# Row maxima and reciprocal sums of an attention kernel sent through DRAM instead of through TensorE transposes

## The chip, the cores and the metric

One core of a Trainium2 chip runs the whole program. The metric is the device time of one execution in microseconds. The engines named below are TensorE (PE; PEld is its weight load), VectorE (DVE), ScalarE (ACT), GpSimd (POOL) and SyncE (SP), whose queue only issues DMAs here. SBUF and PSUM tiles have 128 partitions.

## The reference

The program is a two-layer diffusion backbone over 2048 latent and 256 context tokens. Each layer normalizes, projects to three groups of heads, runs attention, a short convolution and a conformer module, and projects back. The part that matters here is the attention and the gate that follows:

```python
def one_block(qi):
    s = jnp.einsum('bqhd,bkhd->bhqk', qi, k).astype(jnp.float32) * sm_scale
    p = jax.nn.softmax(s, axis=-1).astype(v.dtype)
    return jnp.einsum('bhqk,bkhd->bqhd', p, v)
...
y_a = attn * jax.nn.silu(g_a)
...
return jnp.concatenate([y_a, y_b, y_c], axis=-1)
```

There are 8 heads of 96 numbers for a query or key (64 plus 32 rotary) and 64 for a value. Latent queries attend to all 2304 tokens, context queries to the 256 context tokens only. In the last layer only latent queries are needed.

## The kernel before

Products that need full precision are made of two halves of each operand (a rounded high part and the rest), three matmuls for one product. A layer runs in stages: tokens, features, `attention`, `project`. The order of instructions on every engine is set ahead of time by a scheduler that works on priorities and on its own estimates; a block written inside `tc.high_priority` comes earlier than the code around it.

**Attention.** The work is cut into blocks of one head and 512 queries: 32 per layer, and in layer 0 one more of 256 context queries per head. For each block the key tiles come in pairs. The scores stand with keys on partitions and queries along the row (`sc`, three matmuls, L1073 to L1075), ScalarE makes the exponentials twice (L1076, L1077), GpSimd makes the low half (L1078), and TensorE multiplies with the values (`po`, L1100, L1101). VectorE adds the exponentials up (`acc`, L1085).

The exponent needs the maximum of each query's scores. `prepare` finds it: for each of a block's four tiles of 128 queries, and each of five stretches of keys (four of 512, one of 256), a matmul `pmax` puts queries on partitions (L985) and VectorE reduces along the row (L986); `finish` takes the negated maximum of the five (L989). The result stands as one number per partition. The score matmul wants it as a row, since row 96 of `Q` is multiplied by a row of ones in `K`. So `turn` multiplies the tile `mx`, whose column 96 holds the maxima and whose other columns are zero, by the identity (L994, four matmuls `pmt`) and ScalarE copies partition 96 of the result into row 96 of `Q` (L995). `pmax` has two PSUM buffers, and `pmt` shares one with the transposes below.

`ahead` deals these steps out over the pairs of the block before: LEAD says how many pairs early. They have a higher priority than the pairs. `load` brings `K`, `Q` and the values of the next head on POOL's queue.

When a block is finished, `close` (L1103 on) copies `acc` and `po` out of PSUM, stores `po` to `o_d` on SP's queue (L1108), turns `acc` by four transposes (`psum_t`, L1113), reduces (L1115) and writes the reciprocal of each query's sum into the tile `rinv` (L1116), again one number per partition.

**Projection.** `prepare_y` makes the operand of the output projection for a block of 512 tokens. For each pair of heads it loads `yr`, `ylo` and `yg` on SP's queue (the two halves of the attention's output and the gate), spreads the reciprocals of two heads over 64 columns each (`rr`, ScalarE, L1174), transposes them (`prr`, TensorE, L1175), and VectorE adds the halves (L1176), multiplies by the reciprocals (L1177) and by the gate (L1178). The first block of `prepare_y` is written at a high priority and runs into the end of the attention. In layer 0, SP's queue also issues the 512 KB loads of modulation weights (`wm`) during attention.

## Time and profile before

| | us |
|---|---|
| median of 3 runs | 3695.93 |
| lowest and highest | 3688.89, 3696.3 |
| the profiled execution, time | 3695.0 |
| the profiled execution, span | 3693.2 |
| TensorE busy | 3529.8 (96%) |
| VectorE busy | 2888.8 (78%) |
| POOL busy | 2341.6 (63%) |
| ScalarE busy | 2166.7 (59%) |
| mean granted clock of TensorE | 0.978 of full |

All rows below come from the profiled execution. Its span runs from the first to the last instruction; its time has 1.8 us more around that. Layer 0's attention lies at about 740 to 1600 us, layer 1's at about 2640 to 3400. A busy time of TensorE is made from modelled ends of pipelined matmuls; the cost of a matmul is read from the distance between starts.

### The profile page before, as it was taken

The numbers are of one execution on the slowest core, as the hardware profiler recorded it, in microseconds if no ns is written. First come the engines' busy times: TensorE is split into PE (matmuls) and PEld (weight loads), VectorE is DVE, ScalarE is ACT, GpSimd is POOL, SyncE is SP. The second block draws the span as 40 slices with busy tenths as digits, with TensorE's granted clock in tenths as the row PEclk, the third lists the DMA queues.
The fourth block names the chain that finished last, engine by engine and source line by source line (L and its number), as shares of the span: only waits on it lengthen the run. The fifth ranks groups of instructions, "written<-read, shape, count | busy, mean of one in ns | idle before, by whom it ended". The sixth has DMA issues, their size and how long they took to land. (4 is left out here: it accounts for less than half of the span.)

```text
span 3693.2 us, 52810 instructions
## 1 busy us (share of the span) xinstructions
PE 3529.8 (96%) x17532; PEld 2916.9 (79%) x17532; DVE 2888.8 (78%) x5472; ACT 2166.7 (59%) x4328; POOL 2341.6 (63%) x1497
## 2 busy tenths in 40 slices
PE   7899999999999999999999989999999999998999
PEld 5787888887888787877788878887777777776777
DVE  5986977877888888888437878769988888888832
ACT  4665343247778777877445663433677777776720
POOL 4664344348888888877435654444687887877721
PEclk8999999999999999999999999999999999999999
DMA  7567333433333213312776773435232202222163
GB/s 219 171 186 205 82 107 110 113 112 78 79 79 88 61 45 82 85 58 64 232 231 207 215 213 100 114 99 125 80 76 61 41 27 61 59 61 75 43 197 114
DMA packets 394386, 411.47 MB, mean 111 GB/s; under 512 B 19168, under 2 KB 332128, under 8 KB 388960
## 3 DMA queue, kind: packets, MB, share of 16 engines
q1 hardware_dynamic: 387712, 333.87, 31.2%
q0 software_dynamic: 6400, 74.22, 8.9%
q8 instruction: 138, 2.26, 0.3%
q14 instruction: 136, 1.11, 0.1%
HBM read 266.72 MB, written 141.59 MB: 111 GB/s over the span
## 5 line engine op out<-in xcount | busy, mean ns | idle before, releaser
L1078 POOL TENSOR_TENSOR pl<-p,ph 128x1024 fp32r<-128x1024 f32 (+1 forms) x584 | 1387.2, 2397 | 276.2 <-ACT ph L1077 110.4
L986 DVE TENSOR_REDUCE mx<-pmax 128x1 fp32r<-128x512 f32 (+1 forms) x1296 | 795.1, 628 | 122.0 <-PE pmax L985 113.6
L1076 ACT ACTIVATE p<-sc 128x512 f32<-128x512 f32 x1168 | 713.4, 612 | 240.5 <-PE sc L1075 232.7
L1085 DVE TENSOR_TENSOR acc<-acc,p 128x512 f32<-128x512 f32 x1096 | 756.7, 690 | 55.9 <-ACT p L1076 29.5
L1077 ACT ACTIVATE ph<-sc 128x512 fp32r<-128x512 f32 x1168 | 703.8, 612 | 20.1 <-PE po L1100 16.2
L194 PE MATMUL pf<-hhf,wh 128*128 128x256 f32 (+1 forms) x1584 | 549.3, 348 | 18.2 <-ACT tg L867 8.4
L196 PE MATMUL pf<-hhf,wl 128*128 128x512 f32 (+1 forms) x1584 | 546.4, 347 | 4.5 <-POOL wl L191 3.7
L195 PE MATMUL pf<-hlf,wh 128*128 128x256 f32 (+1 forms) x1584 | 547.2, 346 | 0.0
L985 PE MATMUL pmax<-K,Q 96*128 96x512 f32 (+1 forms) x1296 | 465.0, 386 | 34.8 <-DVE mx L986 26.8
L1073 PE MATMUL sc<-Q,K 97*128 97x512 f32 x1168 | 476.5, 408 | 11.7 <-ACT ph L1077 9.3
L1101 PE MATMUL po<-pl,Vt 128*128 128x512 f32 x1168 | 467.9, 401 | 2.1 <-POOL pl L1078 1.8
L1074 PE MATMUL sc<-Q,K 96*128 96x512 f32 x1168 | 465.2, 398 | 0.0
L1100 PE MATMUL po<-ph,Vt 128*128 128x512 f32 x1168 | 461.9, 396 | 1.1 <-DMA Vt<-v_d 0.8
L1075 PE MATMUL sc<-Q,K 96*128 96x512 f32 x1168 | 462.4, 396 | 0.0
L191 POOL TENSOR_TENSOR wl<-wraw,wh 128x1024 fp32r<-128x1024 f32 x104 | 253.8, 2441 | 292.8 <-ACT wh L190 279.4
L747 DVE SCALAR_TENSOR_TENSOR cacc<-z,hv,cacc 128x384 f32<-128x384 f32 (+5 forms) x780 | 403.0, 561 | 14.3 <-ACT cacc L742 11.2
L194 PEld LDWEIGHTS pf<-hhf,wh 128*128 128x128 f32 x1584 | 303.7, 192 | 57.2 <-ACT wh L190 9.1
L196 PEld LDWEIGHTS pf<-hhf,wl 128*128 128x128 f32 x1584 | 303.0, 192 | 44.3 <-POOL wl L191 7.2
L985 PEld LDWEIGHTS pmax<-K,Q 96*128 96x128 f32 x1296 | 245.3, 190 | 116.9 <-DVE mx L986 58.6
L195 PEld LDWEIGHTS pf<-hlf,wh 128*128 128x128 f32 x1584 | 303.8, 192 | 36.1
L1073 PEld LDWEIGHTS sc<-Q,K 97*128 97x128 f32 x1168 | 222.2, 190 | 71.3 <-ACT ph L1077 20.0
L1075 PEld LDWEIGHTS sc<-Q,K 96*128 96x128 f32 x1168 | 224.5, 192 | 51.5
(257 smaller groups left out, 6189.0 us busy)
## 6 DMA issues: line engine op xcount, KB each, us to landing
wraw<-in_w_in SPq DMA_DIRECT2D x108, 512.0 KB
q_d<-sg SPq DMA_DIRECT2D x68, 384.0 KB
wm<-in_w_mod SPq DMA_DIRECT2D x46, 512.0 KB
v_d<-vs SPq DMA_DIRECT2D x36, 512.0 KB
kn_d<-sg SPq DMA_DIRECT2D x72, 256.0 KB
K<-kn_d POOLq DMA_DIRECT2D x16, 1152.0 KB, 8.5
Vt<-v_d POOLq DMA_DIRECT2D x16, 1152.0 KB, 14.8
o_d<-o SPq DMA_DIRECT2D x64, 256.0 KB
```

What stands on the lines that cost most here:

```text
L194: PE.matmul(out_, lhsT=ahi, rhs=bhi, start=first, stop=False)
L195: PE.matmul(out_, lhsT=ahi, rhs=blo, start=False, stop=False)
L196: PE.matmul(out_, lhsT=alo, rhs=bhi, start=False, stop=last)
L985: PE.matmul(pm[:, :w], lhsT=Q[0:QK, s // P + t, 0], rhs=K[0:QK, a // P : (a + w) // P, 0], start=True, stop=True)
L986: V.tensor_reduce(part[:, t, c : c + 1], pm[:, :w], axis=AX.X, op=ALU.max)
L1073: PE.matmul(sc[:, :n], lhsT=K[0:97, kt, 0], rhs=Q[0:97, qt, 0], start=True, stop=False)
L1075: PE.matmul(sc[:, :n], lhsT=K[0:QK, kt, 1], rhs=Q[0:QK, qt, 0], start=False, stop=True)
L1076: S.activation(p[:, z, :n], sc[:, :n], AF.Exp, scale=scale)
L1077: S.activation(ph[:, z, :n], sc[:, :n], AF.Exp, scale=scale)
L1078: G.tensor_tensor(pl[:, :, :n], p[:, :, :n], ph[:, :, :n].bitcast(F32), op=ALU.subtract)
L1085: V.tensor_tensor(acc[:, :n], acc[:, :n], p[:, z, :n], op=ALU.add)
L1101: PE.matmul(po[:, :n], lhsT=Vt[:, kt0 + z, :], rhs=pl[:, z, :n], start=False, stop=final and z == 1)
```

## The change

The maxima no longer pass through TensorE. `finish` writes them to a tile `mn` of 128 partitions x 4, SP's queue writes these 512 numbers to a row of a DRAM tensor `m_d`, one number of 4 bytes at a time, and then reads the row into `Q`. LEAD goes from 3 to 4. The reciprocals go to a small tile `ri` and by SP's queue into `r_d` in DRAM; `prepare_y` reads a row of it into 64 partitions, twice, as `rb`. The sum of the halves and its product with `rb` now stand in PSUM (`py`). The zeroed columns of `mx` are not needed any more.

```diff
-    mx = [cst.tile([P, 4, 97], F32R, name=f"mx{i}") for i in range(2)]
...
+    mx = [(cst.tile([P, 4, 5], F32, name=f"mx{i}"), cst.tile([P, 4], F32R, name=f"mn{i}")) for i in range(2)]
...
+    m_d = [dr.tile([H, NT], F32, name=f"m_d{l}") for l in range(DEPTH)]
+    r_d = [dr.tile([H, NT], F32, name=f"r_d{l}") for l in range(DEPTH)]
...
             def finish():
-                V.tensor_reduce(m[:, 0:nq, 96:97], part[:, 0:nq, 0 : len(keys)], axis=AX.X, op=ALU.max, negate=True)
+                V.tensor_reduce(m[:, 0:nq], part[:, 0:nq, 0 : len(keys)], axis=AX.X, op=ALU.max, negate=True)
 
             def turn():
-                px = psum("b" if early else "e", "pmt")
-                for t in range(nq):
-                    PE.matmul(px[0:97, t * P : (t + 1) * P], lhsT=m[:, t, :], rhs=idr, start=True, stop=True)
-                S.copy(Q[96:97, s // P : (s + n) // P, 0], px[96:97, :n].rearrange("p (a t) -> p a t", t=P))
+
+                row = m_d[l][h, s : s + n]
+                nc.sync.dma_start(row.rearrange("(t p) -> p t", p=P), m[:, 0:nq].bitcast(F32))
+                nc.sync.dma_start(Q[96:97, s // P : (s + n) // P, 0].bitcast(F32), row.rearrange("(o t p) -> o t p", o=1, p=P))
...
-        LEAD = 3
+        LEAD = 4
...
-                    V.reciprocal(rinv[l][:, s // P : s // P + nq, h], sm[:, :nq])
+                    ri = tp.tile([P, 4], F32, tag="ri", name="ri", bufs=2)
+                    V.reciprocal(ri[:, :nq], sm[:, :nq])
+                    nc.sync.dma_start(r_d[l][h, s : s + n].rearrange("(t p) -> p t", p=P), ri[:, :nq])
...
-                    px = psum("b" if bi == 0 else "cde"[k % 3], "prr")
-                    for t in range(n // P):
-                        rr = rp.tile([P, 2, 64], F32, tag="rr", name="rr", bufs=RR)
-                        S.copy(rr, rinv[l][:, s // P + t, 2 * k : 2 * k + 2].unsqueeze(2).to_broadcast([P, 2, 64]))
-                        PE.transpose(out=px[:, t * P : (t + 1) * P], in_=rr.rearrange("p a b -> p (a b)"), identity=idn)
-                    V.tensor_tensor(r[:, :n], r[:, :n], lo[:, :n], op=ALU.add)
-                    V.tensor_tensor(r[:, :n], px[:, :n], r[:, :n], op=ALU.mult)
-                    V.tensor_tensor(r[:, :n], r[:, :n], g[:, :n], op=ALU.mult)
+                    rb = rp.tile([P, 512], F32, tag="rb", name="rb", bufs=2)
+                    for z in range(2):
+                        nc.sync.dma_start(rb[64 * z : 64 * z + 64, :n], r_d[l][2 * k + z : 2 * k + z + 1, s : s + n].to_broadcast([64, n]))
+                    px = psum("b" if bi == 0 else "cde"[k % 3], "py")
+                    V.tensor_tensor(px[:, :n], r[:, :n], lo[:, :n], op=ALU.add)
+                    V.tensor_tensor(px[:, :n], px[:, :n], rb[:, :n], op=ALU.mult)
+                    V.tensor_tensor(r[:, :n], px[:, :n], g[:, :n], op=ALU.mult)
```

The order on the engines moves with it. In the new code the maxima matmul is L980, the score matmul L1068, the value matmuls L1095 and L1096, the transposes of the sums L1108; a count at a row's end (x4) stands for equal rows in sequence.

On TensorE, before, at a boundary of blocks in layer 1: the narrow `pmax` is the last of its block, and the first `sc` of that block stands at the end.

```order
L985 MATMUL pmax<-K,Q 128x256
L985 MATMUL pmax<-K,Q 128x512 x2
L994 MATMUL pmt<-idr,mx_89 97x128 x4
L985 MATMUL pmax<-K,Q 128x512
L1073 MATMUL sc<-Q,K 128x512
```

The same kind of place in the changed kernel, also layer 1.

```order
L980 MATMUL pmax<-K,Q 128x256
L1108 MATMUL psum_t<-idr,accs 128x128 x4
L980 MATMUL pmax<-K,Q 128x512 x2
L1096 MATMUL po<-pl,Vt 128x512
L1095 MATMUL po<-ph,Vt 128x512
L1096 MATMUL po<-pl,Vt 128x512
L980 MATMUL pmax<-K,Q 128x512 x2
L980 MATMUL pmax<-K,Q 128x256
L980 MATMUL pmax<-K,Q 128x512 x2
L1068 MATMUL sc<-Q,K 128x512
```

The turns are gone, and with the larger LEAD more of the next block's `pmax` and three value matmuls stand between a block's last `pmax` and its first `sc`.

On TensorE of the changed kernel there is a longer run of `pmax` in layer 1, ahead of the second block of every second head; this is its end.

```order
L980 MATMUL pmax<-K,Q 128x512 x2
L1096 MATMUL po<-pl,Vt 128x512
L1095 MATMUL po<-ph,Vt 128x512
L1096 MATMUL po<-pl,Vt 128x512
L980 MATMUL pmax<-K,Q 128x512 x2
L980 MATMUL pmax<-K,Q 128x256
L980 MATMUL pmax<-K,Q 128x512 x4
L980 MATMUL pmax<-K,Q 128x256
L980 MATMUL pmax<-K,Q 128x512
L1068 MATMUL sc<-Q,K 128x512
```

With the rows ahead of these, sixteen `pmax` of the block after stand between a block's last `pmax` and its first `sc`.

On SP's queue of the changed kernel, in layer 1's attention: `m_d<-mn` is the write of the maxima, `Q<-m_d` the read of the row, `r_d<-ri` the store of the reciprocals.

```order
L1113 DMA r_d_114<-ri 128x4x1
L989 DMA m_d_112<-mn_92 128x4x1
L1103 DMA o_d_106<-o 128x512
L990 DMA Q<-m_d_112 1x4x128
L1113 DMA r_d_114<-ri 128x4x1
L989 DMA m_d_112<-mn_90 128x4x1
L990 DMA Q<-m_d_112 1x4x128
L1113 DMA r_d_114<-ri 128x4x1
L1103 DMA o_d_106<-o 128x512
```

Before, SP's queue held only the stores of `o_d` there; now the write and the read stand in it, with a store between them at some blocks.

## Rows read from the trace of the kernel before

**Rows 1.** The page's part 1: busy us (share) and instructions by engine.

```profile
PE 3529.8 (96%) x17532; PEld 2916.9 (79%) x17532; DVE 2888.8 (78%) x5472; ACT 2166.7 (59%) x4328; POOL 2341.6 (63%) x1497
```

**Rows 2.** Windows: length, busy PE, PEld, DVE, ACT, POOL, clock, DMA.

```profile
740.00:1600.00 860.00, 854.76 (x4272) 693.94 (x4271) 738.15 (x1364) 637.18 (x1186) 708.78 (x329) 1.00 0.31 76
2640.00:3500.00 860.00, 835.70 (x3638) 660.64 (x3638) 757.06 (x1272) 643.78 (x1238) 683.16 (x311) 0.98 0.24 57
3390.00:3400.00 10.00, 7.79 (x22) 6.17 (x23) 8.01 (x11) 3.53 (x7) 3.67 (x2) 0.66 0.42 120
```

**Rows 3.** Waits in 2749 to 3373: us in total, times, longest.

```profile
PEld pmax L985 <- DVE mx L986: 21.9, 61, 0.6
PEld sc L1073 <- ACT Q L995: 2.0, 5, 0.4
```

**Rows 4.** Timeline of PE, layer 1: start us, us, instruction.

```profile
3020.69 0.28 PE L985 MATMUL pmax<-K,Q 96*128 96x256 f32 x1
...
3021.83 0.49 PE L994 MATMUL pmt<-idr,mx 128*97 128x128 f32 x4
3022.20 0.50 PE L1101 MATMUL po<-pl,Vt 128*128 128x512 f32 x1
...
3022.99 0.40 PE L985 MATMUL pmax<-K,Q 96*128 96x512 f32 x1
3023.23 0.40 PE L1073 MATMUL sc<-Q,K 97*128 97x512 f32 x1
...
3024.87 0.60 PE L1113 MATMUL psum_t<-idr,accs 128*128 128x128 f32 x4
3025.22 0.48 PE L1073 MATMUL sc<-Q,K 97*128 97x512 f32 x1
```

**Rows 5.** Lines: out<-in, count, busy us, mean ns, idle before and releaser.

```profile
L994 PE MATMUL pmt<-idr,mx 128*97 128x128 f32 x272 | 33.9, 245 | 0.4 <-DVE mx L989 0.3
L1175 PE MATMUL prr<-idr,rr 128*128 128x128 f32 x136 | 29.5, 276 | 3.9 <-ACT rr L1174 3.9
```

**Rows 6.** Timelines of VectorE and TensorE, end of layer 1.

```profile
3386.46 5.36 DVE L1176 TENSOR_TENSOR yr<-yr,ylo 128x512 f32<-128x512 f32 x1 [1.46 <-DMA yr<-o_d]
...
3392.21 0.79 PE L985 MATMUL pmax<-K,Q 96*128 96x512 f32 x1 [5.03 <-DVE mx L986]
3392.80 0.63 PE L1101 MATMUL po<-pl,Vt 128*128 128x512 f32 x1
3393.23 0.63 PE L1100 MATMUL po<-ph,Vt 128*128 128x512 f32 x1
```

**Rows 7.** Timeline of VectorE at the boundary of group 4.

```profile
3019.79 1.65 DVE L986 TENSOR_REDUCE mx<-pmax 128x1 fp32r<-128x512 f32 x3
3021.47 0.18 DVE L989 TENSOR_REDUCE mx<-mx 128x4 fp32r<-128x20 f32 x1
```

**Rows 8.** Timelines of SP's queue and ScalarE at the program's opening.

```profile
0.75 0.39 SPq L106 DMA_DIRECT2D rinv<-in_c  x1
2.12 4.11 SPq L228 DMA_DIRECT2D wm<-in_w_mod  x4
2.56 1.28 ACT L124 ACT_TABLE_LOAD   x1 [2.56 <-DMA rinv<-in_c]
```

**Rows 9.** The chain that ended last: start us, us, step.

```profile
3559.06 3.22 DMA yr<-o_d
```

**Rows 10.** Timeline of SP's queue, layer 0's features: stores and loads.

```profile
348.08 0.38 SPq L875 DMA_DIRECT2D sgc_d<-tg  x1
351.81 0.33 SPq L806 DMA_DIRECT2D sgcl<-sgc_d  x1
...
421.62 0.34 SPq L811 DMA_DIRECT2D y_d<-sgcl  x1
423.33 0.34 SPq L806 DMA_DIRECT2D sgcl<-sgc_d  x1
```

**Rows 11.** The page's part 3: queue, packets, MB, share of engines.

```profile
q1 hardware_dynamic: 387712, 333.87, 31.2%
```

More of the change, by code (lines that the diff above doesn't have):

```diff
@@ L139, in trunk @@
     rcol = rinv[1][:, :, 0:1]
-    mx = [cst.tile([P, 4, 97], F32R, name=f"mx{i}") for i in range(2)]
-    zero = rinv[0].rearrange("p t h -> p (t h)")[:, :97]
-    G.memset(zero, 0.0)
-    for t in mx:
-        for i in range(4):
-            G.tensor_copy(t[:, i], zero)
+    mx = [(cst.tile([P, 4, 5], F32, name=f"mx{i}"), cst.tile([P, 4], F32R, name=f"mn{i}")) for i in range(2)]
     kn_d = [dr.tile([H, NOPE, NTT, 2, P], F32, name=f"kn_d{l}") for l in range(DEPTH)]
@@ L973, in prepare @@
             keys = [(a, min(512, NT - a)) for a in range(k0 * P, NT, 512)]
-            m = mx[count[0] % 2]
-            early = count[0] < NE
+            part, m = mx[count[0] % 2]
             count[0] += 1
-            part = m
             nq = n // P
```

## The prediction

> **What bounds the kernel now.** I read the page's busy times first [rows 1]: TensorE works 96% of the span, VectorE 78%, ScalarE 59%. Such shares average over stages, so I then read windows [rows 2]. In 740 to 1600, layer 0's attention, TensorE is busy 854.8 of 860 us at full clock; in 2640 to 3500, layer 1's, 835.7 with VectorE at 757.1. Both are TensorE's, but in layer 1 VectorE is close. The waits of 2749 to 3373 show how close [rows 3]: TensorE waited 21.9 us for a reduction (L986) to free a PSUM buffer for the next maxima matmul (L985), and only 2.0 us for the row of maxima (`Q`, L995). That is 23 blocks, 0.95 us a block on the first wait. So a matmul removed is worth its time, and a later row of maxima is free only up to the work TensorE has between a block's last maxima matmul and its first score matmul (L1073). I call this work the slack; it decides the forecast.
>
> **What is removed from TensorE.** Starts in order on TensorE give spacings, which are the real cost [rows 4]: the four matmuls that turn the maxima start at 3021.83 and the next at 3022.20, about 0.32 us as I choose it (0.37 here, with some waiting); 512 columns follow each other every 0.235 us, four transposes of the sums take 0.35. 64 blocks of 512 queries x 0.32 + 8 of 256 x 0.16 = 21.8 us (the 272 matmuls of L994 [rows 5]). In the projection 34 groups of four transposes (136, [rows 5]) x 0.36 = 12.2 us. The copies of L995 and L1174 leave ScalarE, at 644 of 860 us in [rows 2] far from the bound: nothing. The wait for the copied row goes, some 3 us over the kernel by scaling [rows 3]. Of the 0.95 us a block of waits for reductions in layer 1, the new order (LEAD 4: preparation runs half a pair further ahead) leaves perhaps half: 32 x 0.47 = 15 us.
>
> **End of layer 1.** Before, VectorE sat in its queue behind L1176, whose operand came late: its add ran 5.36 us, TensorE's next maxima matmul waited 5.0 us, and the clock afterwards was the lower level for a stretch (0.66 granted over 3390 to 3400 [rows 2]; 512 columns then start every 0.43 us instead of 0.235) [rows 6]. 13 such matmuls, an estimate of what that stretch holds, x 0.2 = 2.6 us more. In the new order these adds stand behind the last reductions, so 5.0 + 2.6 go, but they now meet the loads of the broadcast reciprocals, two buffers deep, in the last block; I take back half: 4 us gained, bounded by 0 and 7.6.
>
> **What is added: a chain through DRAM.** Per block it is: last reduction, maximum of five (L989), SP's write of 512 numbers of 4 bytes, its landing, SP's read of that row into `Q`, its landing, score matmul. No operation before is like the write, so I bound it.
> - From the last maxima matmul at 3020.81 (its buffer's start) to the end of L989 at 3021.65: 0.84 us [rows 4, 7].
> - Read: a first load of 8 KB in 128 pieces, issued at 0.75, let ScalarE start at 2.56: 1.8 us [rows 8]. A read of o_d took 3.22 us on the chain of waits [rows 9], 3.6 with its issue: upper end.
> - Write: a 192 KB store and the load that waits for it are issued 1.71 us apart; the longest such pair 3.73 [rows 10]. The new one has 512 pieces, 32 for each of 16 DMA engines, against 8. The queue's packets average 0.312 x 3693.2 x 16 / 387712 = 47.6 ns [rows 11], so 24 more are 1.1 us. Its issue is longer too: loads of 1024 pieces took SP 1.03 us each, of 128 pieces 0.39 [rows 8], which puts 512 at 0.66, 0.3 over a small one. 1.7 + 1.1 + 0.3 = 3.1; low 1.7, high 5.1.
>
> The chain D is then 0.84 + 3.1 + 1.8 = 5.7 us; low 4.3, high 9.5. I take 5.7 as the writes and reads near it in kind are the short ones, outside the crowded projection.
>
> **Slack against chain.** Slack is counted in the new order, at 0.235, 0.12 and 0.35 us a row. Layer 0 has 12.8 to 15.8 us nearly everywhere (8.9 at the least): D is hidden there, and 40 blocks keep their gain. SP also issues layer 0's 512 KB loads, which stand between write and read in places and wait for buffers, but the slack covers them. In layer 1 the order drew the blocks together. Per two heads the eight slacks are 5.4, 16.1, 6.5, 2.6, 4.0, 4.9, 3.3, 3.9; the start has 36.9, 17.7, 10.1, 3.5, the end 3.5, 4.0, 3.1, 2.0. Summing D - slack where positive over the 32 blocks: 16 us at 4.3, 43 at 5.7, 73 at 7.0, 140 at 9.5. SP's order also puts `o_d` or `r_d` stores between write and read in some blocks, queued in front of the read; they are released 1 to 4 us ahead of the score matmul, within D.
>
> Three blocks (slack 6.5, 5.4, 5.4) have a run of sixteen maxima matmuls before the score matmul. Fourteen reductions at 0.60 us (0.33 for the narrow ones), from three in 1.65 us [rows 7], with the sums' reduce, take VectorE 8.8 to 9.7 us: it binds there, 3.2 + 3.4 + 3.4 = 10 us at any D below 9.
>
> A wait also costs clock. After 5.0 us of idling, the 2.6 us above were lost [rows 6]. I charge 2 us, a choice below that, to each stall of 3 us or more and nothing to shorter ones: at 5.7 seven of them, 14 us; at 7.0 twenty, 40; at 9.5 some 50.
>
> In layer 0's features the stores of sga_d stand behind the first head's write and read on SP: 3 us as a choice, 0 to 6. The 72 stores of reciprocals and 72 broadcast loads run beside the projection's own loads, [rows 2] showing DMA engines at 0.24 to 0.31: nothing, if the loads come in time; if not, the last block's multiply waits up to 3.6 us for each of 4 groups, 14 us, kept for the range.
>
> **Sum.** 43 + 10 + 14 + 3 = 70 us lost; 21.8 + 12.2 + 3 + 15 + 4 = 56 gained: +14 us. The profiled execution took 3695.0 us (span 3693.2 and 1.8 around it), 0.9 under the median of 3695.93, so I make no correction: **3709 us**. With the waits for reductions not saved at all it is 3724; with D at 5.2 (33 + 10 + 10 + 3 - 56 = 0) 3695. So its own range is 3695 to 3725.
>
> **Rivals.**
> - **Small pieces cost double** (slower). If a 4-byte piece holds an engine two such packets, the write is 4.2 to 4.4 us and D 7.0. Then 73 + 10 + 40 + 3 - 56 = +70: 3765 us. For it: [rows 11] average larger packets, whose fixed part is unknown, and no row shows a write of 4 bytes. Against it: eight pieces to an engine already lie in the 1.71 us. The loss passes 0.2% (7 us) from D about 5.5. The Trainium skill, "DMA: Bandwidth & Descriptors", "Rules for kernel authors" and "Specifications", says that a strided last dimension becomes one descriptor per element and that below 512 bytes the engine reads, modifies and writes; by that rule this rival is what happens, and no run here shows it yet.
> - **The chain is short** (faster). If the pieces overlap, so that the write costs no more than the shortest store seen, D is 4.3 and the loss 16 + 10 + 6 + 3 = 35, less 56: -21, 3674 us; with the remaining waits for reductions gone, 3662. For it: each piece is small and 16 engines share them. The same page's "Anatomy of one DMA" puts a fixed cost of about 2.0 us on a DMA, mostly the receipt of the write; two of these with the 0.84 us would make D an estimated 4.8 and the sum 24 + 10 + 8 + 3 - 56 = -11, 3684.
> - **VectorE takes TensorE's time back** (no change). In layer 0 [rows 2] VectorE has 738 us of work to TensorE's 855, so not there; in layer 1 [rows 2] it could keep all of the 15 us; with D at 4.8 the sum is then 24 + 10 + 8 + 3 - 41 = +4: 3699 us.
> - **The change doesn't free TensorE**: the removed matmuls were hidden beside waits, so their 34 us are no gain. [rows 2] with 99% busy at full clock in layer 0 speak against it; the time would be 3743.
>
> **Chances.** My forecast 0.38; small pieces 0.11; hidden matmuls 0.04; short chain 0.32; VectorE keeping the time 0.15. The measurement can tell about 0.2% (7.4 us) from no change. Faster: the short chain's 0.32 and 0.04 of VectorE's case: 0.36. Slower: the 0.15 of the two dear cases and 0.28 of the forecast's 0.38: 0.43. Within: the forecast's other 0.10 and 0.11 of VectorE's case, 0.21. The range reaches from the short chain's 3662 to the double pieces' 3765 and 3 us of sga_d's upper end: 3662 to 3768.
>
> **What would show it.** In the changed profile, the score matmul's weight load or matmul in layer 1 waits for a DMA of `Q` from `m_d`: some 22 waits, 40 us or so in total, the longest near 4 us. The time from the issue of the write to that of the read tells the 3.1 us, and from the read's issue to the score matmul the 1.8. Layer 0 should lose nothing on that wait and end some 12 to 15 us earlier; the waits of maxima matmuls on reductions in layer 1 should lie between 10 and 25 us; granted clock in layer 1 falls slightly under 0.98. If the write to read takes 2 us, the rival of the short chain holds; over 4, the double pieces. I am wrong in kind if layer 0 shows the wait, or if the projection's multiply waits for `rb`.

## The result

The changed kernel takes 4118.22 us (median of 5 runs, 4115.43 to 4121.38) where the kernel before, now with 5 runs, takes 3694.96 us: a ratio of 1.1151 (95% interval 1.1135 to 1.1167), 423 us or 11.5% slower. The forecast was 3709 us, the range ended at 3768.

The page of the changed kernel, part 1, which answers to [rows 1]:

```profile
PE 3573.6 (87%) x17124; PEld 2941.5 (71%) x17124; DVE 2863.3 (70%) x5472; ACT 2102.2 (51%) x4120; POOL 2337.3 (57%) x1488
```

TensorE is busy 44 us longer although some 400 of its instructions are gone, and its share falls from 96% to 87%. So it waited some 380 us more, and what it did went at a lower clock. The windows tell where. I cut both kernels at the first and last score matmul of each layer, which sets the stretches of attention named above right; first the kernel before, layer 0's attention and layer 1's (columns as in [rows 2]):

```profile
812.00:1737.30 925.30, 908.20 (x4430) 727.09 (x4429) 803.78 (x1455) 716.71 (x1359) 790.07 (x359) 0.99 0.30 76
2598.80:3499.10 900.30, 871.23 (x3796) 687.70 (x3795) 791.42 (x1324) 667.53 (x1284) 708.57 (x325) 0.99 0.24 58
```

and the changed kernel, the same two stretches:

```profile
812.00:1795.50 983.50, 910.51 (x4271) 726.31 (x4270) 791.99 (x1454) 689.69 (x1299) 787.66 (x360) 0.96 0.46 73
2674.40:3921.40 1247.00, 922.35 (x3651) 720.07 (x3651) 781.57 (x1325) 655.12 (x1235) 709.17 (x326) 0.85 0.27 43
```

Layer 0's attention is 58 us longer, layer 1's 347; the stretch between them 17, the ends 1. In layer 1 TensorE is busy 51 us more at a clock of 0.85 for 0.99, and idle 325 us for 29. The waits of the changed kernel over the whole run (total, times, longest), in the place of ScalarE's row in [rows 3]:

```profile
PE sc L1068 <- DMA Q<-m_d: 341.7, 35, 20.9
```

In time order I count 27 such waits in layer 1, 291.6 us, and 8 in layer 0, 50.1 us. So layer 0 shows the wait, which the prediction had named as a sign of being wrong in kind. Its other such sign came too, the multiply of the projection waiting for `rb`:

```profile
DVE py L1173 <- DMA rb<-r_d: 28.9, 15, 4.4
```

SP's own waits tell which half of the chain it is. The read of the row (L990) waits for the write to land:

```profile
SPq L990 <- DMA m_d<-mn: 655.0, 72, 25.4
```

That is 9.1 us a block, where the prediction had 3.1 from the write's issue to the read's. One block in a quiet stretch of layer 1, on SP's queue, TensorE and VectorE:

```profile
3205.00 0.36 SPq L989 DMA_DIRECT2D m_d<-mn  x1
3213.49 0.56 SPq L990 DMA_DIRECT2D Q<-m_d  x1
3203.10 0.28 PE L980 MATMUL pmax<-K,Q 96*128 96x256 f32 x1
...
3216.76 0.77 PE L1068 MATMUL sc<-Q,K 97*128 97x512 f32 x1 [6.88 <-DMA Q<-m_d]
3204.81 0.16 DVE L984 TENSOR_REDUCE mn<-mx 128x4 fp32r<-128x20 f32 x1
```

The last maxima matmul starts at 3203.10, the maximum is done at 3204.97, the write is issued at 3205.00, the read 8.49 us later, the score matmul 3.27 us after that: 13.7 us in all. The DMA rows of the window from the write's issue to the read's (40 slices of 0.21 us, then the queue's packets, MB and share) show what the write did:

```profile
DMA  0000560000000000000000000000000000000000
...
q1 hardware_dynamic: 528, 0.00, 3.0%
```

All 528 packets go through the engines in the fifth and sixth slice, about 0.9 to 1.3 us after the issue, for 3% of the window. Then nothing moves for 7 us, and the write is still not reported as landed. And beside the loads of the next head (POOL's queue, SP's, TensorE):

```profile
3125.93 0.54 POOL L960 DMA_DIRECT2D K<-kn_d  x1
...
3127.81 0.36 SPq L989 DMA_DIRECT2D m_d<-mn  x1
...
3156.29 0.56 SPq L990 DMA_DIRECT2D Q<-m_d  x1
3159.99 0.79 PE L1068 MATMUL sc<-Q,K 97*128 97x512 f32 x1 [20.92 <-DMA Q<-m_d]
```

The same write, issued 1.9 us after such loads began, is followed by the read after 28.5 us; the score matmul waited 20.9 us. Seven waits of layer 1 are of this size, 16.2 to 20.9 us; the others are 2.9 to 11.7. At six of the seven the next head's loads had begun 1 to 2 us before the write or began 0.5 us behind it; at three the write took 23.5 to 28.5 us, at three the read 11.6 to 12.7. The seventh has no such load within 20 us:

```profile
2931.16 0.58 SPq L990 DMA_DIRECT2D Q<-m_d  x1
...
2941.57 0.80 PE L1068 MATMUL sc<-Q,K 97*128 97x512 f32 x1 [16.25 <-DMA Q<-m_d]
```

Its read took 10.4 us, with a store of `r_d` issued between its write and the read, and one of `o_d` behind.

In layer 0 the maximum waits for SP as well. At one of its eight waits it was ready at 1201.6, and SP was held by a store:

```profile
1192.07 14.15 SPq L1103 DMA_DIRECT2D o_d<-o  x1
...
1206.79 0.58 SPq L989 DMA_DIRECT2D m_d<-mn  x1
```

At five of the eight the write was issued 4.3 to 5.4 us after the maximum was there, and the read followed 10.8 to 13.3 us behind it; TensorE had 12.5 us of work left when the maximum was ready.

### The profile page after: what moved, and what is told of

It is laid out like the page before. It is cut to its first block, busy times and chain, and to the rows that moved or that the text cites. A ratio compares the mean times of both kernels' runs of the same rounds, so it can differ in the third digit from the quotient of the medians.

```text
span 4116.5 us, 52377 instructions
## 1 busy us (share of the span) xinstructions
PE 3573.6 (87%) x17124; PEld 2941.5 (71%) x17124; DVE 2863.3 (70%) x5472; ACT 2102.2 (51%) x4120; POOL 2337.3 (57%) x1488
## 4 chain that ended last, share of the span: by engine, by line
PE 60%; DMA 20%; DVE 11%; issue 4%; ACT 3%; POOL 1%; SPq 1%; DVEq 0%; ACTq 0%; POOLq 0%
DMA m_d<-mn 10%; PE sc L1068 7%; PE sc L1069 6%; PE sc L1070 6%; PE po L1095 5%; PE pmax L980 5%; PE po L1096 5%; PE pf L193 5%; PE pf L195 5%; PE pf L194 5%; DMA Q<-m_d 3%; PE pout L193 2%; PE pout L195 2%; PE pout L194 2%; DVE cacc L746 2%
## 5 line engine op out<-in xcount | busy, mean ns | idle before, releaser
L981 DVE TENSOR_REDUCE mx<-pmax 128x1 f32<-128x512 f32 (+1 forms) x1296 | 795.5, 628 | 171.2 <-PE pmax L980 163.9
L1068 PE MATMUL sc<-Q,K 97*128 97x512 f32 x1168 | 501.6, 429 | 372.3 <-DMA Q<-m_d 341.7
L1068 PEld LDWEIGHTS sc<-Q,K 97*128 97x128 f32 x1168 | 236.9, 203 | 444.7 <-DMA Q<-m_d 323.4
L980 PE MATMUL pmax<-K,Q 96*128 96x512 f32 (+1 forms) x1296 | 476.3, 395 | 25.4 <-DVE mx L981 18.6
L1069 PE MATMUL sc<-Q,K 96*128 96x512 f32 x1168 | 488.4, 418 | 0.0
L1070 PE MATMUL sc<-Q,K 96*128 96x512 f32 x1168 | 484.7, 415 | 0.0
L1096 PE MATMUL po<-pl,Vt 128*128 128x512 f32 x1168 | 470.0, 403 | 1.1 <-POOL pl L1073 1.1
L1095 PE MATMUL po<-ph,Vt 128*128 128x512 f32 x1168 | 466.3, 399 | 0.0
L980 PEld LDWEIGHTS pmax<-K,Q 96*128 96x128 f32 x1296 | 252.3, 196 | 116.2 <-DVE mx L981 57.6
L1078 DVE COPY acc<-p 128x512 f32<-128x512 f32 (+1 forms) x72 | 47.7, 662 | 370.6 <-ACT p L1071 351.8
```

Of the source, the lines that this page charges most:

```text
L980: PE.matmul(pm[:, :w], lhsT=Q[0:QK, s // P + t, 0], rhs=K[0:QK, a // P : (a + w) // P, 0], start=True, stop=True)
L981: V.tensor_reduce(part[:, t, c : c + 1], pm[:, :w], axis=AX.X, op=ALU.max)
L1068: PE.matmul(sc[:, :n], lhsT=K[0:97, kt, 0], rhs=Q[0:97, qt, 0], start=True, stop=False)
L1069: PE.matmul(sc[:, :n], lhsT=K[0:QK, kt, 0], rhs=Q[0:QK, qt, 1], start=False, stop=False)
L1070: PE.matmul(sc[:, :n], lhsT=K[0:QK, kt, 1], rhs=Q[0:QK, qt, 0], start=False, stop=True)
```

## The experiments

Two theories stood for the long landing: the count of pieces, and pieces that share a line of memory; a third asked for their size. A further question was what makes seven waits of layer 1 twice as long as the rest, the next head's loads or SP's order. A time given without an interval is of one execution; executions of the kernel before went from 3676.5 to 3706.2 us in all.

**Small DMAs by themselves.** A kernel of only such transfers, each `write; read; copy` waited for:

```
nc.sync.dma_start(d.rearrange("(t p) -> p t", p=P), src[:, :4])   # adjacent
nc.sync.dma_start(row, d); V.tensor_copy(src[0:1, 0:1], row[0:1, 0:1])
```

> This kernel leaves the whole model out and stores a tile of ones; it only sends small DMAs one after another, each a write to DRAM from SBUF, a read of what was written, and a VectorE copy that the next write waits for. In the changed kernel the read of the row is issued 8.3 us after the write in a quiet stretch, although the 528 packets have all passed the DMA engines 1.4 us after the write's issue. Theory 1, the pieces land one after another at one place in memory: time from write to read falls in proportion to their number, about 1.5 us + 13 ns a piece: 512 pieces 8.3 us, 256 pieces 4.9, 128 pieces 3.2, 64 pieces 2.4, 16 pieces 1.8. Theory 2, any piece below a minimum size has a fixed long way: about 8 us for each count of 4-byte pieces and for 128 runs of 16 bytes, and under 2.5 us for 128 runs of 512 bytes. Theory 3, pieces that share a line of memory wait for each other: 512 pieces 64 bytes or 512 bytes apart land in about 2 to 3 us, 512 pieces next to each other in 8.3, and 128 runs of 64 bytes in about 2. Two writes of 512 pieces sent together: by theory 1 the first read is issued after about 8 to 15 us and the second after 15; by theory 2 both after about 8.5. A read scattered into 512 pieces of 4 bytes of SBUF: 2 to 3 us if only DRAM writes are slow.

Rows of SP's queue and of VectorE's copies that end a chain; `full` is the kernel's write, `gapsmall` the same 512 numbers 64 bytes apart, `row<-src` a row sent inside SBUF in 128 runs of 16 bytes:

```profile
25.68 0.36 SPq L110 DMA_DIRECT2D full<-src  x1
34.38 0.23 SPq L105 DMA_DIRECT2D row<-full  x1
37.95 0.14 DVE L99 COPY src<-row 1x1 f32<-1x1 f32 x1 [12.29 <-DMA row<-full]
142.31 0.39 SPq L121 DMA_DIRECT2D gapsmall<-src  x1
144.22 0.21 SPq L122 DMA_DIRECT2D row<-gapsmall  x1
145.49 0.14 DVE L99 COPY src<-row 1x1 f32<-1x1 f32 x1 [3.21 <-DMA row<-gapsmall]
199.30 2.59 SPq L154 DMA_DIRECT2D row<-src  x2
201.25 0.14 DVE L99 COPY src<-row 1x1 f32<-1x1 f32 x1 [1.98 <-DMA row<-src]
```

Adjacent numbers: 8.70 us from write to read, and 3.57 more to the copy. 64 bytes apart: 1.91. Inside SBUF: 1.95 from issue to copy, complete. With 512 pieces of 4 bytes both times, neither the number of pieces nor their size alone sets the time. Runs of 16, 64 and 512 bytes, one to a partition and also adjacent, took 1.4 to 2.4 us. Sent from ScalarE's queue, the adjacent write took 8.7 us as well. The count misses as well: 256, 128 and 64 adjacent pieces took 7.8 to 8.6 us, 7.4 to 7.6 and 6.0 to 6.5, where the first theory had 4.9, 3.2 and 2.4. The very first write of the program took 10.3 us. Of two writes sent together the first had landed after 8.7 to 8.8 us, and the second held its own read up no further. A read scattered into 512 pieces took about 4.3.

**Spacing, partitions and company.** The same kind of kernel.

> Again the whole model is left out; small DMAs one after another, each waited for. In the first such run 512 pieces of 4 bytes next to each other took 8.3 to 8.7 us from write to read and the read then 3.5 us, the same pieces 64 bytes apart 1.9 us. Theory (pieces that share a 64-byte line wait for each other): 8 bytes apart, 8 sharers, about 5 us; 16 bytes apart, 4 sharers, 3; 32 bytes apart, 2 sharers, 2.3; 64 bytes apart 1.9. Rival (the line that counts is longer, 512 bytes or the whole 2 KB): 8 to 32 bytes apart still 7 to 8 us. One column of 8, 16, 32, 64, 128 partitions, next to each other: if the number of sharers of a line sets it, 16 partitions and more are alike, 6 to 7.5 us, and 8 about 3; if the number of lines, rising with each. Reading the same row three times after the write: if the read is slow since the lines are still being put right, the first takes 3.5 us and the next two 1.3; if the lines themselves stay slow, all 3.5. Beside a 2 MB load on another queue: 512 adjacent pieces about 10 to 11 us to the read; the row sent inside SBUF in 128 runs of 16 bytes, 1.95 us when quiet, 4 to 7 us; pieces in lines of their own 4 to 7 us: if the load's share of the engines is what delays, all gain the same 2 to 4 us.

512 numbers 8, 16 and 32 bytes apart, write and read on SP's queue:

```profile
17.96 0.36 SPq L126 DMA_DIRECT2D gapviii<-src  x1
22.50 0.23 SPq L127 DMA_DIRECT2D row<-gapviii  x1
23.90 0.36 SPq L126 DMA_DIRECT2D gapxvi<-src  x1
26.54 0.23 SPq L127 DMA_DIRECT2D row<-gapxvi  x1
27.95 0.36 SPq L126 DMA_DIRECT2D gapxxxii<-src  x1
29.95 0.23 SPq L127 DMA_DIRECT2D row<-gapxxxii  x1
```

4.54, 2.64 and 2.00 us; with 8.3 to 8.9 for adjacent ones and 1.9 at 64 bytes this is a smooth fall with the number of neighbours. One column of 8, 16, 32, 64 and 128 partitions took 1.15, 1.35, 3.3 to 4.4, 6.6 to 6.9 and 7.0 to 7.7 us, so it also rises with the number of adjacent pieces, which sharing of one 64-byte line alone doesn't say. Partitions are not what counts: 64 pieces took 6.6 to 6.9 us from 64 partitions and 6.0 to 6.5 from 16. Of three reads of a fresh row the first took 3.3 to 3.7 us, the next two 1.4 to 1.7, as if what is slow were still going on when the first read starts. The sums point the same way: from the issue of the write to the end of the first read, 11.8 to 12.3 us passed each time that all 512 adjacent numbers were sent, also for the write of 10.3 us, whose read then took 1.8.

Beside a 2 MB load that was issued 0.3 to 0.5 us behind it, the adjacent write took 9.9 to 11.6 us. A row sent inside SBUF took 1.9, and a write with numbers 64 bytes apart 2.2 to 2.4, nearly as when quiet: a miss, I had expected 4 to 7 for both. Reads issued 1 to 2 us into the load took 4.4 to 5.8 us for 1.3 to 2.7. So a quick DMA issued just ahead of a load got through, and one behind its start did not. How wide a line is, and who waits in it, these runs don't tell, nor whether it counts that pieces further apart also lie in more memory. That the small distance of 4-byte pieces is the cause, they do tell.

**One part alone.** Reciprocals by DMA, maxima by transposes (the part's own lines of the diff, LEAD 3):

> The kernel before with the reciprocals alone sent through DRAM (stores of r_d, broadcast loads of rb, product in PSUM); maxima by transposes, LEAD 3. Theory (the maxima's chain costs all of the loss): the 34 groups of transposes are gone, 12 us, and nothing waits in attention; 3675 to 3693 us. Rival (the reciprocals' stores and loads cost too, since 512-piece stores stand in the queue ahead of the projection's loads): 3700 to 3730 us, with a wait of the multiply by rb of 5 us or more at the end of each layer.

3704.4 us, ratio 1.0030 (1.0013 to 1.0047): the rival, if mildly; the multiply's waits for `rb` were 4.5 us at the longest, where it had 5 or more. In the profiled execution attention gained 3 and 10 us, but the stretch from layer 0's last score matmul to layer 1's first lost 13 and the end 8. Its waits (total, times, longest):

```profile
DVE xo L1209 <- DMA xo<-in_xT: 54.0, 14, 8.8
PE pout L196 <- DVE xo L1209: 24.3, 8, 9.3
```

Before, the first of these rows was 4.5 us and TensorE's wait for `xo` 2.3. So the loads of the projection's residual come late, and the transposes saved are paid back there; that the broadcast loads ahead of them in SP's queue do it is argued, not shown. Maxima by DMA, reciprocals by transposes:

> The changed kernel with the reciprocals by transposes as before. Theory (the maxima's write sets the time, and a reciprocals' store issued just behind it or before it adds its own landing): 4118 less some 30 to 90 us: the stalls of 16 to 21 us in layer 1 (seven, of 126 us in total) shrink to 7 to 10 us where a store of r_d stood between write and read; 4030 to 4090 us. Rival (those long stalls come from the next head's loads of keys and values alone): they stay, 4118 + 12 = 4130 us.

4096.8 us: the maxima hold 404 of the 423 us. Neither number was met. The six long waits beside loads stayed, as the rival had it (15.6 to 19.7 us); the seventh, without loads, fell to 9.2, which speaks for a part of the stores of `r_d` in that one, as the theory had it. 21 us were gained.

**More lead.** `LEAD = 4` to `LEAD = 9`.

> The changed kernel with LEAD 9 for 4. Counted in its order, layer 0's slack between a block's last maxima matmul and first score matmul goes from 12.8 to 15.8 to 27 us or more, layer 1's stays (2.0 to 5.0 us mostly). Theory (the row comes 12 to 25 us after the last maxima matmul, and layer 0's loss is that alone): layer 0's eight waits for the row (50 us) vanish and its attention takes 58 to 70 us less; layer 1 stays; 4045 to 4065 us. Rival (layer 0 lost its time to clock or to the DMA load as such): under 20 us gained, 4100 us or more.

4131.8 us, the rival's number; layer 0 kept seven waits, 51.5 us in all, although its slack doubled. SP's queue shows why, at one of them:

```profile
1185.33 0.53 SPq L989 DMA_DIRECT2D m_d<-mn  x1
1187.43 9.25 SPq L202 DMA_DIRECT2D wm<-in_w_mod  x1
1196.77 10.12 SPq L1103 DMA_DIRECT2D o_d<-o  x1
1206.99 0.39 SPq L1113 DMA_DIRECT2D r_d<-ri  x1
1213.87 0.56 SPq L990 DMA_DIRECT2D Q<-m_d  x1
```

Between the write of 1185.33 and its read at 1213.87 stand a 512 KB load whose issue alone holds SP 9.25 us and a store that holds it 10.12, both while the next head's loads (POOL's queue, issued 1182 to 1190) fill the engines. Yet SP is free again at 1207.4, and the read waits 6.5 us more for the write to land. So the write ends last: issued 3.2 us after the loads began, it takes 28.5 us, as in layer 1, against a slack of 27. With LEAD 4 the writes of these blocks were issued 20 us and more after the loads began. Starting earlier moved them into the loads.

**Numbers a line apart.** `m_d` of `[H, NT, 16]` with one number in 16 used, the read as four DMAs; else as the kernel with maxima alone:

> The changed kernel's way through DRAM for the maxima, with each number in a 64-byte line of its own in m_d (and the read as four DMAs of 128 pieces of 4 bytes); reciprocals by transposes as before. Beside it stands the same kernel with the numbers next to each other, 4096.8 us. Theory (pieces that share a line land slowly): write to read about 1.9 to 2.5 us instead of 8.3, the read some 3 to 4 us, the row 6 to 7 us after the last maxima matmul; stalls of 60 to 100 us in layer 1, 3740 to 3800 us. Rival (any write of 512 pieces to DRAM is slow in this kernel): write to read stays above 7 us and the time above 4050 us.

3824.2 us for 4096.8, on the theory's side, 24 us above its range. (The read differs too, four DMAs for one.) SP's wait for the write, 9.1 us a block in the changed kernel, is

```profile
SPq L991 <- DMA m_d<-mn: 174.5, 72, 15.9
```

2.4 a block. What was left were five waits of 13 to 18 us at heads' boundaries.

**No DRAM at all.** Four DMAs from `mn` into row 96 of `Q`:

```diff
-                nc.sync.dma_start(row.rearrange("(t p) -> p t", p=P), m[:, 0:nq].bitcast(F32))
-                nc.sync.dma_start(Q[96:97, s // P : (s + n) // P, 0].bitcast(F32), row...)
+                for t in range(nq):
+                    nc.sync.dma_start(Q[96:97, s // P + t, 0].bitcast(F32), m[:, t : t + 1].bitcast(F32))
```

> The changed kernel with the maxima sent from the tile mn straight into row 96 of Q, four DMAs of 128 pieces inside SBUF, no DRAM between; reciprocals by transposes as before. Measured alone four such DMAs took 2.7 to 4.0 us, so the row comes 3.5 to 4.8 us after the last maxima matmul, against slack of 2.6 to 6 us in layer 1. Theory (the loss is the time that the write through DRAM takes to land): waits of 0 to 2 us for Q, 10 to 20 us in total, against 22 us of turns and some waits saved: 3665 to 3695 us. Rival (it is the queue: SP is held by stores during each head's loads, whatever is sent): stalls of 5 to 15 us once a head stay, 14 of them, 3740 to 3850 us.

3803.9 us, 1.0304 (1.0278 to 1.0330). And with queries dealt over the tiles, so that one DMA does:

> As the kernel with four DMAs inside SBUF, but the queries of a block are dealt to the four tiles in turn (query 4p+t to partition p of tile t), with Q laid out as all high parts, then all low parts, so that the row is one DMA of 128 runs of 16 bytes; measured alone it took 1.95 us. The row comes 2.8 us after the last maxima matmul: hardly any wait, 3660 to 3685 us by the theory that the DRAM write's landing was the loss; by the rival that SP's queue is held during each head's loads, 3740 to 3850 us.

3763.5 us, 1.0174 (1.0157 to 1.0192). Both are the rival's by time, but not by its cause. There are 92.0 and 50.2 us of waits in layer 1, nearly all in one wait a head. The kernel with one DMA:

```profile
2972.76 0.56 POOL L960 DMA_DIRECT2D K<-kn_d  x1
2975.09 0.48 SPq L989 DMA_DIRECT2D Q<-mn  x1
2986.24 0.80 PE L1067 MATMUL sc<-Q,K 97*128 97x512 f32 x1 [6.74 <-DMA Q<-mn]
```

The row needs 1.95 us alone and 11 us here, issued 2.3 us after the loads began on POOL's queue; SP's queue issues nothing else in the 10 us before it. It isn't SP that is held. This kernel has a price of its own, the strided weight load of its maxima matmuls, 309 ns mean for 190 before:

```profile
L981 PEld LDWEIGHTS pmax<-K,Q 96*128 96x128 f32 x1296 | 386.0, 309 | 107.3 <-DVE mx L982 56.6 <-issue 7.5 <-DVE mrow L216 2.0
```

**Moving the loads as a block.** Started in a head's second block, with one-element copies that wait for its second pair:

```diff
+                if pi == 1 and h + 1 < H and job[0][1] == 512:
+                    load(h + 1, p)
```

> The changed kernel with the next head's loads of keys, queries and values started three blocks later than a head's end would let them, after the first exponentials of the second pair of a head's second block (four one-element POOL copies make the loads wait). In the changed kernel the loads start about 2 us ahead of a head's boundary and take 20 us, and the maxima's write or read that is sent then lands 20 to 28 us later. Theory (a small DMA stands behind the loads' pieces in the engines): the seven waits of 15 to 21 us at heads' boundaries of layer 1 shrink to the 7 to 9 us of the others, and layer 0's eight waits (50 us in total) to under 15: 4118 becomes 3980 to 4050 us. Rival (those waits come from SP's order, stores between write and read): they stay, 4100 to 4130 us.

4160.2 us: a miss, outside both numbers. Layer 1's longest wait fell from 20.9 to 15.1 us, but layer 0 lost another 48 us. With the row inside SBUF:

> The row of maxima sent inside SBUF by four DMAs, reciprocals by transposes, and the next head's loads moved to the second block of a head as in the run beside it. With the loads at the boundary this kernel had six waits of 11 to 15 us (80 us) in layer 1 and 12 of 0.3 to 2 us. Theory: the six shrink to 0 to 2 us, and with the clock that they cost 3804 becomes 3690 to 3712 us. Rival (they are not the loads'): 3790 us or more.

3833.4 us (1.0371), the rival's number: layer 1's long waits fell from 11 to 15 us to 9 to 10, and layer 0 got seven of 6 to 8. With three of a block's four tiles sent ahead of the last:

> As the kernel beside it (row inside SBUF, loads moved), but the maximum of the first three tiles of 128 queries is taken and sent as soon as they are through, and only the last tile's 128 numbers are sent after the last reduction. One such DMA alone takes about 1.5 to 2 us, so the row is complete some 2.5 to 3 us after the last maxima matmul against slack of 1.8 to 4.4 us. Theory: what waits for Q are left sum to under 12 us in layer 1; the 22 us of turns are saved: 3668 to 3692 us, faster than both kernels. Rival (VectorE, which gets one more small reduction a block, or the waits for reductions take it back): 3692 to 3715 us.

3808.7 us (1.0322), a miss of both numbers. The old kernel with only the loads moved:

> The kernel before, maxima and reciprocals by transposes, with only the next head's loads moved as in the runs beside it. It tells what the move is worth without any row sent by DMA: nothing there waits for a small DMA in attention, so 3690 to 3700 us; if the loads at the boundary held something else back, 3670 to 3688.

3699.3 us (1.0018, 0.9997 to 1.0038): nothing. The kernel with early tiles shows the fault in the edit; the third row is the score matmul that waited:

```profile
3046.53 0.55 POOL L963 DMA_DIRECT2D K<-kn_d  x1
3053.22 5.05 SPq L993 DMA_DIRECT2D Q<-mn  x4
3071.24 0.77 PE L1068 MATMUL sc<-Q,K 97*128 97x512 f32 x1 [8.64 <-DMA Q<-mn]
```

The loads, due early in the block, start at 3046.53, in the middle, run some 20 us, and the row is sent into them at 3057 or so. A block lasts 27 us; 20 us of loads find no place in it. I had moved the collision, not taken it away. Six such waits of 8.6 to 9.1 us stood in layer 1; its others for the row were 0.6 us or less.

**No loads.** Heads 2 to 7 compute with the keys, queries and values of heads 0 and 1, so that part of the computation is not the reference's:

> The changed kernel without the loads of keys, queries and values of heads 2 to 7 in either layer: these heads compute with what heads 0 and 1 loaded, the same amount of work on every engine. Theory (the long waits, once a head, are small DMAs that stand behind the 4.9 MB of the next head's loads): layer 1's waits of 15 to 21 us fall to the 8 to 10 us of the others and layer 0's waits of 5 to 8 us vanish but for the first heads: 4118 becomes 3990 to 4050 us. Rival (SP's in-order queue or the write alone): waits as before, 4100 us or more.

4110.0 us, the rival's number, but not as a whole. Layer 0 won back 30 of the 58 us that it had lost. Layer 1's writes were all followed by the read after 8.4 to 11.4 us, none after 23, as the theory had it. Yet layer 1 as a whole took 34 us more: its order was another one, its ordinary waits were mostly longer (9 to 12 us), and six reads took 8.4 to 12.3 us with no load near. (A head's loads sum to 4434 to 4626 KB in the trace, not 4.9 MB.) Two blocks, SP and TensorE:

```profile
3054.06 0.56 SPq L990 DMA_DIRECT2D Q<-m_d  x1
3054.71 0.39 SPq L1103 DMA_DIRECT2D o_d<-o  x1
3055.20 0.38 SPq L1113 DMA_DIRECT2D r_d<-ri  x1
3066.32 0.80 PE L1068 MATMUL sc<-Q,K 97*128 97x512 f32 x1 [18.31 <-DMA Q<-m_d]
3101.77 0.56 SPq L990 DMA_DIRECT2D Q<-m_d  x1
...
3104.75 0.79 PE L1068 MATMUL sc<-Q,K 97*128 97x512 f32 x1 [9.62 <-DMA Q<-m_d]
```

12.3 us from the read's issue at 3054.06 to the score matmul, 3.0 from that at 3101.77, with the same two stores behind each. In the slow one the DMA engines move nothing in the last 8 of the 12.3 us, as after the adjacent write. In the kernel with maxima alone, where no store of `r_d` stands there, no read away from the loads took over 3.9 us. So the reciprocals' stores, 512 adjacent pieces like the maxima, are the suspect; it wasn't tried by itself and stays open.

**Loads cut in three.** Keys, queries and values each in a block of their own, 8 to 12 us long; the row inside SBUF, three tiles early:

> The row of maxima inside SBUF with three tiles sent early, as before, but the next head's loads are cut in three: keys in the second block of a head, queries in the third, values in the fourth, each started after the second pair's first exponentials and some 8 to 12 us long, so that none should be under way when a block's row is sent 5 to 8 us ahead of its end. With the loads in one piece this kernel took 3808.7 us, with five waits of 8.6 to 9.1 us in layer 1 and four of 5.4 to 5.8 in layer 0. Theory: these waits fall under 2 us each and the time to 3670 to 3710 us. Rival (the row is held by something else that comes once a head): they stay, 3780 us or more.

3685.4 us, 0.9976 (0.9966 to 0.9985): layer 1's waits for the row went from 55.1 to 9.6 us, layer 0's from 24.7 to none. One block earlier, and the control with the old transposes:

> The row of maxima sent inside SBUF, three tiles of a block early, with the loads cut in three and one block earlier than in the run before (keys in the first block of a head, queries in the second, values in the third). There, layer 0 waited six times, 12.4 us in all, for queries of the next head. Theory: these waits go and the rest stays, 3685 becomes 3668 to 3680 us, 0.4 to 0.7% faster than the kernel before. Rival (the earlier loads meet other DMAs, the 512 KB loads of layer 0 or the rows): 3683 to 3700.

> The kernel before (maxima and reciprocals by transposes) with only the next head's loads cut in three, keys in a head's first block, queries in its second, values in its third. If the gain of the kernel with the row inside SBUF comes from the turns taken off TensorE, this one stays within 0.2% of the kernel before, 3688 to 3702 us. If the loads' places gave it, 3675 to 3688.

3667.8 us, 0.9932 (0.9913 to 0.9951), and 3671.4, 0.9944 (0.9921 to 0.9967). Both beat the kernel before, and most of it is the loads, against what I expected of the control; what they had held up there I didn't look for. The 3.6 us between the two are within their intervals: the row inside SBUF is worth no more than the turns. Without turns layer 0's attention is 9.7 us shorter than the control's, layer 1's 11.6 longer, 9.0 of it waits for the row.

**The square.** The maxima through DRAM, adjacent, loads cut:

> The maxima through DRAM as in the changed kernel, numbers next to each other, reciprocals by transposes, loads of the next head cut in three and spread over its first three blocks. With the loads in one piece it took 4096.8 us, seven or eight waits of 15 to 20 us among those of 8 to 9. Theory: the long waits fall to those of the rest, write to read 8.4 to 11 us, read 2 to 4, slack about 3.5: 28 waits of 8 to 9 us, 250 us and the clock they cost; 3980 to 4040 us. Rival (loads don't matter to it): 4080 us or more.

and a line apart, loads cut:

> The same with each number in a 64-byte line of its own, loads cut in three. Both causes are gone; the row still goes through DRAM. Write to read 1.9 to 2.5 us, the read 3 to 4, so the row is there 6 to 7.5 us after the last maxima matmul against slack of 4.5 to 7 us: waits of 0 to 2 us in layer 1, 20 to 40 us in all: 3685 to 3715 us. If something else of the way through DRAM costs time, waits of 5 us and more stay and it is above 3740 us.

| maxima through DRAM | loads in one piece | loads cut in three |
|---|---|---|
| numbers adjacent | 4096.8 | 3998.0 |
| numbers a line apart | 3824.2 | 3701.9 |

Both came where expected. Waits of the score matmul for the row (total, times, longest), adjacent and apart, loads cut:

```profile
PE sc L1078 <- DMA Q<-m_d: 271.2, 33, 10.2
```

```profile
PE sc L1079 <- DMA Q<-m_d: 28.0, 27, 1.7
```

From 8.2 us a wait to 1.0. The 404 us split into 273 to 296 for adjacency and 99 to 122 for the loads in one piece; 12 us are left against the kernel before. But cutting the loads also gave 20 us to the kernel with turns. Against that one, 3671.4 us, the best way through DRAM is still 30 us slower, about its 28.0 us of waits.

## Why the prediction was wrong

- **What bounds, and the slack: right.** With D at 12.3 to 13, D less slack sums to 214 to 233 us over 27 blocks of layer 1, by the prediction's own list. Measured were 27 waits, 291.6 us; the rest are the seven long ones, six of which met loads.
- **The write: the step that failed.** It was sized 3.1 us, with 5.1 as the upper end; away from loads layer 1's measured 8.0 to 10.3. The prediction scaled with the time that packets take in the engines [rows 11]. That part was even too high: 0.4 us for 528 packets. The landing of adjacent pieces isn't in any engine's time, and no row of before held it; [rows 10] were stores of long runs. An operation of a kind that the trace doesn't have should have had an end far above its nearest row. This step with the read is about half of the miss: with the write at 8.3 and the read at 3.3 us, D is 12.4, and the prediction's own sum is 217 + 52 (26 stalls) + 3 - 56 = +216 us, an estimate of 3911. The rest is mostly what it put at nothing, layer 0's waits and the loads, and gains that didn't come.
- **The rule weighed in the rival.** The Trainium skill, "DMA: Bandwidth & Descriptors", "Specifications", has the engine read, modify and write below 512 bytes. As a price by size this doesn't agree with the runs: 512 pieces of 4 bytes that lie 64 bytes apart land in 1.9 to 2.0 us, and 128 runs of 16 bytes in 1.4 to 2.4. Whether it is what makes adjacent pieces slow, no run shows. Its "Anatomy of one DMA" says that the wait for the write's receipt "can cause a surprisingly long delay especially when the write target is HBM"; 7 us after the last packet agree with that, and are 3.5 times the 2.0 us that the page has as the whole fixed cost. It fits that figure for DMAs issued by GpSimd; the prediction used it for two on SP's queue without saying so.
- **The rival of small pieces: right in sign, wrong in size and cause.** It held that packets cost twice; they cost less than assumed. Its sign, over 4 us from write to read, came for another reason.
- **The read: 1.8 us, measured 1.8 to 5.3** away from loads, but for the one of 10.4. In most blocks it took 3.3 us or so where it was issued within 8.6 us of the write, and about 1.9 where 9.4 or more had passed: some 12 us from the write's issue either way.
- **From the last maxima matmul to the maximum: 0.84 us, measured 1.9** in the block shown, where VectorE's queue has an add before the last reduction and one behind it. The 3020.81 that the 0.84 starts from stands in no row; [rows 4] have 3020.69, which makes it 0.96.
- **Layer 0 hidden: wrong.** The slack was as counted, but the prediction let it cover SP's waiting. Eight waits, 50 us, came: stores in SP's queue, held up to 14 us, kept the write back, and it then landed in 10.8 to 13.3 us at five of them.
- **What stood between: missed.** The head loads on POOL's queue weren't in the sum at all; in layer 1 they cost a small DMA some 8 to 20 us once a head.
- **Gains.** The turns are worth about what was counted, in layer 0 (9.7 us of 11.5 against the control). The 15 us of waits for reductions did not come: 17.2 us in layer 1's attention by 38 waits, 18.6 before. The 12 us of the projection were paid back by late loads. The 10 us for the runs of sixteen maxima matmuls did not show: at those three blocks the row came last, with waits of 16.5 to 20.9 us. The small terms for the end of layer 1 and for `sga_d` can't be told apart under waits of this size.
- **Small slips in the sums.** By the slacks as printed the sums at D of 4.8 and 5.2 come out 2 to 3 us lower, and the range's 3662 takes 12 us off 3674 where the text has 15 left to save. Nothing hangs on them.
- **Clock.** 2 us a stall was about right, if all of the busier time is put down to the clock (0.85 granted in layer 1 for 0.99): layer 1's 51 us of busier TensorE and the 10 us of turns it no longer does, over 27 waits, make 2.3.

## What to carry to other kernels

Turning a column into a row through DRAM by 4-byte pieces side by side took 12 us from issue to use here, where the turn took 0.3 us of TensorE's time. Pieces 64 bytes apart land in 2 us, and a row sent inside SBUF takes 2 when nothing else moves. Even so, no way by DMA was clearly faster here than the turns with the same loads. Before putting a small DMA on a path with a few us of slack, look for the big loads that run at that moment, on any queue, and cut them so that they end first: even without a small DMA that was worth 0.6% here. Measure the new operation by itself before it is summed.

## What was not expected of the hardware

- A write of 512 adjacent 4-byte pieces from 128 partitions is through the engines after 1.3 us and lands after 8.3 to 8.9; 16 bytes apart it lands after 2.3 to 2.6, 32 bytes apart after 2.0 to 2.1. Of 64 adjacent pieces it makes little difference whether 16 or 64 partitions send them (6.0 to 6.9).
- A first read of such a row takes 3.3 to 3.7 us, a second 1.4 to 1.7.
- A small DMA on SP's queue, issued 2.3 us after 3.3 MB of loads were started on POOL's, landed after 11 us for 1.95 alone, so another queue was no way past them. Issued 0.3 us ahead of a 2 MB load, such a row took 1.9.
- With such loads under way, the issue of a store of 256 KB held SP's queue 14.15 us, and in another kernel 10.12.
- A weight load of TensorE with columns four 4-byte numbers apart took 309 ns for 190.
